# Hybrid attention and SSD layer: how the weights that combine three attention branches reach GpSimd

## The chip, the cores and the metric

The kernel runs on one core of a Trainium2 chip. The core has a matrix engine (PE, with its weight loads PEld), a vector engine (DVE), a scalar engine (ACT), GpSimd (POOL) and a sync engine (SP) that only issues DMAs; ACT and POOL can issue DMAs too, each in the order of its own queue. The metric is the device time of one execution in microseconds (us), the median of several runs.

## The reference, cut to what matters

One decoder layer, sequence 2048, width 1024, all in float32. A projection of the input gives queries, keys and values for 16 attention heads of size 64, two gates, and the inputs of a state-space mixer (SSD). Attention is computed three times, with dilations 1, 4 and 16, each over a window of 128 steps with a linear bias; each branch d gives an output o_d and a log-sum-exp l_d for every position and head. The three are combined:

```
o1, l1 = dilated_window_attention(q, k, v, slopes, DILATIONS[0])
o2, l2 = dilated_window_attention(q, k, v, slopes, DILATIONS[1])
o3, l3 = dilated_window_attention(q, k, v, slopes, DILATIONS[2])
wts = jax.nn.softmax(jnp.stack([l1, l2, l3], axis=0), axis=0)
y_att = wts[0] * o1 + wts[1] * o2 + wts[2] * o3
```

The result is gated and normalised, as is the SSD's; both are concatenated, multiplied by one output matrix, added to the input, and layer-normalised.

## The kernel before

**Stages.** First come the projections and the SSD (to 1168.5 us), which leave q, k, v, the gates and the SSD's output (d_us) in DRAM. Then the attention, 487.6 us, which the change is in, and the output projection, 383.9 us.

**Attention.** The loop runs over 8 pairs of heads (`pr`), and in each over 24 steps: three branches (`d` = 0, 1, 2), four quarters (`qd`), two halves. It is written as a pipeline by hand: iteration i issues `scores` of step i (matrix products into S, on DVE a fused bias, scale and row minimum, L945, and on ACT the exponential with its row sum, L951), `transposes` of step i-2 (PE to T, copied by DVE), and `values` of step i-3 (PE to N). After each second half, N is copied to `num`, the unnormalised output of the branch (L1016, L1019, L1022, all on ACT). Behind these stand, by the tables `STEPS` and `LOADS` and the conditions around them, jobs that are due at the step `at` = step i-3: loads for this pair and the next, and the combining of the pair before. The orders of PE, DVE, ACT and POOL are exactly those in which the program issues; only SP's queue is put in order by a planner.

**Statistics and weights.** Row minima and sums are gathered in a small tile. `statistics` transposes them and SP writes them to DRAM (d_st, L1038 to L1048), its last part at step (2,3,1). `gather` (L1050), a DMA on POOL's queue, reads them back as `cm`. In the next pair, at (0,2,1) and (0,3,0), `weights` makes the three softmax weights from cm: minimum, difference and exponential (part 0, L1057 to L1060), then products, sums, reciprocal (part 1, L1063 to L1067), all on DVE but the exponential. SP writes them to d_wd (L1068).

**Combining.** `combine(A, k)`, k from 0 to 5, works on tiles of 128 x 2048 elements, on POOL for pairs 0 to 6 and on DVE for the last. Steps 0, 1 and 3 broadcast the weights of a branch from d_wd to a tile `wb`, one row of 8 KB to 64 partitions, twice (L1081, on SP), and multiply `num` into it (L1083); steps 2 and 4 add (L1087); step 5 multiplies by the gate (L1098) and writes d_ua. Their places are in STEPS: 0 at (1,0,0), 1 at (1,1,0), 2 at (1,2,0), 3 at (1,3,0), 4 at (2,1,0), 5 at (2,2,0). Behind them POOL issues the next pair's loads: q, k (L862), v and vs (L878, L880). SP issues all six broadcasts as soon as d_wd has landed, since wb has three buffers. Then `permute` (L904, L908) copies the next pair's queries to the orders of branches 1 and 2, and the gather comes behind it in POOL's queue.

**Output projection.** 32 blocks, of the SSD's half (br = 1) and the attention's (br = 0), each multiplied with two halves of the output matrix: 64 products. Every block is first split in a high and a low part: `split` casts on ACT (L1141) and subtracts on DVE, for the very first block on POOL (L1143). `squares` makes its row sums for the norm (L1148, L1151). The first block's split is issued at (2,0,1) and (2,1,0) of the last pair. The weights of the last pair are made behind the attention (`weights(A, 0)`, `weights(A, 1)`), ahead of the loop over the products; the third block is split after product one, behind them in the order of ACT and DVE.

Of the kernel before, what the change touches and what calls it, by code (L numbers as in the profile page):

```python
# [9 lines left out]
F32 = mybir.dt.float32  # L10
# [6 lines left out]
S = 2048  # L17
# [11 lines left out]
def hybrid_layer(ctx, tc, xb, xc, w52, wv, wdt, convw, convb, dtb, alog, dskp, gcol, wout,  # L29
# [5 lines left out]
    def dap(t, off, ap):  # L35
        return bass.AP(tensor=t.tensor, offset=t.offset + off, ap=ap)
# [805 lines left out]
    with ExitStack() as c2:  # L842
# [137 lines left out]
        def values(A, d, qd, half, pts):  # L980

            pt, pc = pts
            if half == 0:
                if qd == 0:
                    A["num"].append(cm_.tile([128, NR, NJ], F32, name="num", bufs=6))
                A["N"] = [psN.tile([128, 512], F32, name=f"N{i}") for i in range(2)]
            num, v, vs = A["num"][d], A["v"][d], A["vs"].get(d)
            at = lambda bq: 4 * bq + qd if d == 1 else 4 * qd + bq
            out = lambda i, h, lo, hi: A["N"][i][64 * h:64 * h + 64, 128 * half + lo:128 * half + hi]

            def mm(o, l, r, start):
                nc.tensor.matmul(o, l, r, start=start, stop=True, skip_group_check=True)  # L992
            for i in range(2):
                m = at(2 * i + half)
                if first(d, qd, 2 * i + half):
                    for h in range(2):
                        mm(out(i, h, 0, 128), v[:, m, 64 * h:64 * h + 64], pt[:, h, i], half == 0)
                    continue
                for a in range(2):
                    for h in range(2):  # L1000
                        w = (v, vs)[a != i][:, m - (a == i == 0 or a != i), 64 * h:64 * h + 64]
                        mm(out(i, h, 64 * a, 64 * a + 64), w, pt[:, h, i, 64 * a:64 * a + 64], half == 0 and a == 0)
            for a in range(2):
                for i in range(2):
                    m, rows = at(2 * i + half), slice(64 * i, 64 * i + 64)
                    if first(d, qd, 2 * i + half):
                        continue
                    for h in range(2):
                        w = v[rows, m - i] if a == i else vs[rows, m - 2 * i]
                        mm(out(i, h, 64 * a, 64 * a + 64), w[:, 64 * h:64 * h + 64],  # L1010
                           pc[rows, h, 64 * a:64 * a + 64], False)
            if half == 1:
                for i in range(2):
                    nm = A["N"][i][:, 0:256]
                    if d == 0:
                        nc.scalar.copy(f2(num[:, 4 * qd + 2 * i:4 * qd + 2 * i + 2, :]), nm)  # L1016
                    elif d == 1:
                        o = num.rearrange("p (b s) (n a j) -> p n b a s j", b=4, a=2, j=16)[:, qd, 2 * i:2 * i + 2]
                        nc.scalar.copy(o, nm.rearrange("p (b a s j) -> p b a s j", b=2, a=2, s=4))  # L1019
                    else:  # L1020
                        j = 8 * (4 * qd + 2 * i)
                        nc.scalar.copy(num[:, :, j:j + 16].rearrange("p r (n j) -> p n r j", j=4),  # L1022
                                       nm.rearrange("p (n r j) -> p n r j", r=16, j=4))
# [28 lines left out]
        def weights(A, part):  # L1052

            m_, s_ = A["cm"][:, :, 0], A["cm"][:, :, 1]
            if part == 0:
                mm = A["mm"] = cm_.tile([128, 32], F32, name="mm")
                nc.vector.tensor_tensor(mm, m_[:, 0], m_[:, 1], op=OP.min)  # L1057
                nc.vector.tensor_tensor(mm, mm, m_[:, 2], op=OP.min)
                nc.vector.tensor_tensor(m_, mm[:, None, :].to_broadcast([128, 3, 32]), m_, op=OP.subtract)
                nc.scalar.activation(m_, m_, AF.Exp)  # L1060
                return
            mm = A["mm"]
            nc.vector.tensor_tensor(s_, s_, m_, op=OP.mult)  # L1063
            nc.vector.tensor_tensor(mm, s_[:, 0], s_[:, 1], op=OP.add)
            nc.vector.tensor_tensor(mm, mm, s_[:, 2], op=OP.add)
            nc.vector.reciprocal(mm, mm)
            nc.vector.tensor_tensor(m_, m_, mm[:, None, :].to_broadcast([128, 3, 32]), op=OP.mult)  # L1067
            nc.sync.dma_start(dap(d_wd[A["pr"]], 0, [[32, 128], [2 * S, 3], [1, 32]]), m_)  # L1068

        def combine(A, k):  # L1070

# [4 lines left out]
            pu = lambda a: a.rearrange("p (n r j) -> p r n j", r=NR, j=8)  # L1076
            if k in (0, 1, 3):
                d = k - k // 2
                wb = A["wb"] = cm_.tile([128, NR, NJ], F32, name="wb", bufs=3)
                for h in range(2):  # L1080
                    nc.sync.dma_start(f2(wb[64 * h:64 * h + 64]),  # L1081
                                      dap(d_wd[pr], (d * 2 + h) * S, [[0, 64], [1, S]]))
                eng.tensor_tensor(wb, A["num"][d], wb, op=OP.mult)  # L1083
                if k == 0:
                    A["acc"] = wb
            elif k < 5:
# [107 lines left out]
        def norm(n):  # L1194
# [10 lines left out]
            if n == 15:  # L1205
                for s in (slice(0, 512), slice(512, D)):
# [9 lines left out]

        O = {}
        pairs = {}
        STEPS = {(0, 0, 0): (None, "v", 0, 2), (0, 0, 1): (None, "vs", 0, 2), (1, 0, 0): (0, "q", 1),
                 (1, 1, 0): (1, "k", 1), (1, 2, 0): (2, "v", 1, 0), (1, 3, 0): (3, None, 0), (2, 0, 0): (None, "v", 1, 1),  # L1220
                 (2, 1, 0): (4, "vs", 1, 1), (2, 2, 0): (5, None, 0)}
        LOADS = {(0, 0, 0): ((8, None, "k_0"),), (1, 0, 1): ((9, None, "q_0"),), (1, 1, 0): ((10, None, "ex"),),
# [3 lines left out]
        todo = [(pr, d, qd, half) for pr in range(8) for d in range(3) for qd in range(4) for half in range(2)]  # L1226
        pts = {}
        TA = 2
# [1 line left out]
        with tc.manual_schedule(engines={E.PE, E.DVE, E.Activation, E.Pool}):  # L1230
            for i in range(len(todo) + TA + 1):
# [22 lines left out]
                if i > TA:  # L1254
# [5 lines left out]
                        statistics(pairs[pr], 1)  # L1260
                        gather(pairs[pr])
                    at = d, qd, half
                    if pr and at in ((0, 2, 1), (0, 3, 0)):
                        weights(pairs[pr - 1], qd - 2)
                    if at == (0, 0, 0) and pr < 7:
                        pairs[pr + 1] = load_pair(pr + 1)
                    if pr and at == (0, 3, 0):
# [42 lines left out]
            squares(0, 1)  # L1310
            split(1, 1)
            squares(1, 1)
            weights(A, 0)
            weights(A, 1)
            ops = [(n, 1) for n in range(4)] + [(n, 0) for n in range(4)]
            ops += [(n, br) for n in range(4, 16) for br in (1, 0)]
            items = [(4 * j + k, hf) for j in range(2) for k, hf in
# [5 lines left out]
            for i, (k, hf) in enumerate(items):  # L1323
# [19 lines left out]
                if i in splits:  # L1343
                    j = splits[i]
                    split(*ops[j])
                    squares(*ops[j])
                    for m in (j + 2,) if 4 < j < 30 else ():
                        fetch_raw(*ops[m])
                    if j >= 7 and j + 1 < 32 and ops[j + 1][1]:
                        residual(ops[j + 1][0])  # L1350
                        scaled(ops[j + 1][0])
# [97 lines left out]
```

## Time and profile before

| | us |
|---|---|
| median of 3 runs | 2043.36 (2038.81 to 2046.38) |
| profiled execution, its time | 2042.05 |
| its span, first to last instruction | 2040.3 |
| PE busy | 1961.6 (96%) |
| DVE busy | 1268.3 (62%) |
| ACT busy | 1125.5 (55%) |
| POOL busy | 1038.0 (51%) |
| mean granted clock | 0.986 |

A row of a group names the line, engine and operation, the tiles written and read, the shapes, the count, then busy time, mean duration in ns, and the idle time of the engine just before, with what ended it. A row of a timeline has start, duration, engine, line, operation, tiles, shape and count, and in brackets the idle time before it with its releaser. A row of the chain of waits has start, duration and what the time went to. "q" behind an engine's name is its queue.

### The profile page before, as it was taken

Reading aid. Unit: us, or ns where it says so; the run is one execution under the profiler, and the core shown is the slowest. Engines: PE = TensorE matmul, PEld = TensorE weight load, DVE = VectorE, ACT = ScalarE, POOL = GpSimd, SP = SyncE. Lnnn points to the kernel's source line nnn. Section 1 sums busy time; section 2 is a strip of 40 time slices with the busy share of each in tenths; the row PEclk is TensorE's granted clock in tenths of the full one; section 3 lists DMA queues with packets and bytes.
Section 4 is the critical chain, followed back from the end, with each engine's and each line's share of the span. In section 5 each row is a group of like instructions: output and inputs, shape, how many; then the busy total and the mean of one; then the engine's idle time right before and its main releaser. Section 6 shows DMA issues by size and latency. Waiting matters only on the chain.

```text
span 2040.3 us, 42723 instructions
## 1 busy us (share of the span) xinstructions
PE 1961.6 (96%) x16024; PEld 1598.5 (78%) x16024; DVE 1268.3 (62%) x3181; ACT 1125.5 (55%) x3067; POOL 1038.0 (51%) x881
## 2 busy tenths in 40 slices
PE   7999999999999999999999999999998889999998
PEld 6788888888888888988888766676666668888886
DVE  7455464677775666644454377887777756665553
ACT  4455443466565766456566488887878742222220
POOL 3466623666655667255655433668766662432222
PEclk8999999999999999999999999999999989999999
DMA  7478695466878777988888856777877799323220
GB/s 273 156 265 284 227 334 195 132 197 192 244 249 301 253 248 258 328 260 268 268 272 263 273 195 166 217 231 230 235 226 220 192 319 301 122 96 105 84 67 31
DMA packets 231150, 447.72 MB, mean 219 GB/s; under 512 B 40288, under 2 KB 112480, under 8 KB 219936
## 3 DMA queue, kind: packets, MB, share of 16 engines
q1 hardware_dynamic: 138928, 189.59, 29.5%
q0 software_dynamic: 43776, 160.49, 23.3%
q10 hardware_dynamic: 48240, 94.92, 15.1%
q8 instruction: 126, 2.06, 0.4%
q14 instruction: 80, 0.66, 0.1%
HBM read 301.91 MB, written 151.39 MB: 222 GB/s over the span
## 4 chain that ended last, share of the span: by engine, by line
PE 85%; DVE 5%; ACT 4%; DMA 3%; issue 2%; POOL 0%; SPq 0%; ACTq 0%; POOLq 0%; DVEq 0%
PE pp L251 13%; PE pp L255 13%; PE pp L253 13%; PE N L992 6%; PE S L939 5%; PE S L1175 4%; PE S L1177 4%; PE S L1176 4%; PE T L966 4%; PE pp L300 3%; ACT P L951 3%; PE ss L300 2%; PE T L1175 2%; PE T L1176 2%; PE T L1177 2%
## 5 line engine op out<-in xcount | busy, mean ns | idle before, releaser
L208 POOL TENSOR_TENSOR w<-wr,w 128x512 fp32r<-128x512 f32 x224 | 294.8, 1327 | 223.3 <-ACT w L207 195.1
L951 ACT ACTIVATE P<-P,st 128x192 f32<-128x192 f32 (+1 forms) x768 | 322.0, 421 | 71.7 <-DVE st L945 66.8
L243 ACT COPY ev<-pp 128x512 f32<-128x512 f32 x200 | 116.9, 587 | 318.1 <-PE pp L255 281.7
L945 DVE CUSTOM_DVE_ANT_0 P<-S,tb 128x192 f32<-128x192 f32 (+1 forms) x768 | 206.4, 324 | 101.6 <-PE S L939 72.6
L263 DVE TENSOR_TENSOR ev<-pp,ev 128x512 f32<-128x512 f32 x152 | 101.1, 686 | 147.9 <-PE pp L255 96.0
L1083 POOL TENSOR_TENSOR wb<-num,wb 128x2048 f32<-128x2048 f32 x21 | 95.5, 4549 | 114.7 <-DMA wb<-d_wd 65.5
L207 ACT CAST w<-wr 128x512 fp32r<-128x512 f32 x224 | 133.5, 619 | 22.0 <-issue 7.5
L951 ACT ACTIVATION_READ_ACCUMULATOR P<-P,st 128x1 f32 x768 | 144.3, 188 | 0.0
L992 PE MATMUL N<-PT,v 128*64 128x64 f32 (+1 forms) x1536 | 126.2, 261 | 11.8 <-ACT num L1016 8.5
L968 DVE COPY PT<-T 128x512 f32<-128x512 f32 x192 | 131.8, 686 | 4.4 <-PE T L966 4.4
L966 PE MATMUL T<-ident,P 128*128 128x128 f32 x768 | 128.4, 291 | 1.5 <-DVE st L945 1.2
L966 PEld LDWEIGHTS T<-ident,P 128*128 128x128 f32 x768 | 82.2, 143 | 49.2 <-issue 22.8
L939 PE MATMUL S<-k,ex 64*64 64x192 f32 (+1 forms) x2048 | 113.7, 333 | 5.8 <-issue 5.8
L202 DVE TENSOR_TENSOR wr<-wr 128x512 f32<-128x512 f32 x128 | 111.3, 870 | 11.3 <-DMA wr<-w 7.5
L992 PEld LDWEIGHTS N<-PT,v 128*64 128x64 f32 x1536 | 78.9, 138 | 49.5 <-issue 18.8
L454 DVE SCALAR_TENSOR_TENSOR ss<-U,cw,ss 128x512 f32<-128x512 f32 x144 | 106.0, 751 | 2.9 <-ACT ss L450 0.6
L1151 DVE TENSOR_REDUCE tb<-P 128x128 f32<-128x1024 f32 x30 | 60.2, 2005 | 45.4 <-ACT P L1148 23.0
L1213 POOL TENSOR_TENSOR k<-k,wb 128x1024 f32<-128x1024 f32 x8 | 25.8, 3225 | 122.5 <-DVE k L1212 122.5
L939 PEld LDWEIGHTS S<-k,ex 64*64 64x64 f32 x2048 | 69.2, 139 | 18.1 <-issue 11.8
L580 ACT ACTIVATE mt<-csb,cs 128x128 f32<-128x128 f32 x256 | 78.5, 393 | 0.9 <-PE ss L620 0.8
L589 DVE TENSOR_TENSOR mt<-mt,ss 128x1024 f32<-128x1024 f32 x32 | 39.0, 1219 | 54.6 <-ACT mt L585 54.3
L251 PE MATMUL pp<-TB11h,w 128*128 128x512 f32 x176 | 69.6, 395 | 0.0
(478 smaller groups left out, 6032.6 us busy)
## 6 DMA issues: line engine op xcount, KB each, us to landing
wr<-w ACTq DMA_DIRECT2D x164, 256.0 KB
d_wc<-w SPq DMA_DIRECT2D x48, 512.0 KB
w<-d_wc POOLq DMA_DIRECT2D x48, 512.0 KB, 6.2
wb<-d_wd SPq DMA_DIRECT2D x48, 512.0 KB
d_wo<-wot POOLq DMA_DIRECT2D x32, 512.0 KB, 4.3
csb<-d_cs ACTq DMA_DIRECT2D x32, 512.0 KB
v<-d_v POOLq DMA_DIRECT2D x16, 1024.0 KB, 6.8
vs<-d_v POOLq DMA_DIRECT2D x16, 960.0 KB, 8.6
```

The lines of the kernel that those rows point to most:

```text
L207: nc.scalar.copy(h, r)
L208: nc.gpsimd.tensor_tensor(l, r, h.bitcast(F32), op=OP.subtract)
L251: nc.tensor.matmul(ps, w[:, 0, k], th[:, k], start=start and k == 0, stop=False, skip_group_check=not start)
L253: nc.tensor.matmul(ps, w[:, 0, k], tl[:, k], start=False, stop=False, skip_group_check=not start)
L255: nc.tensor.matmul(ps, w[:, 1, k], th[:, k], start=False, stop=(k == 3), skip_group_check=not start)
L939: nc.tensor.matmul(o, A["q"][d][64 * h:64 * h + 64, blk, 64 * a:64 * a + 64], kv, start=True, stop=True)
L945: nc.vector.tensor_tensor_reduce(P[:, h, cs], sp[h][:, cs], t, -0.125, 3.0e38, OP.add, OP.min, accum_out=stat(A, 0, d, h, blk))
L951: nc.scalar.activation(p, p, AF.Exp, bias=stat(A, 0, d, h, blk), scale=-1.0, accum_out=stat(A, 1, d, h, blk))
L966: nc.tensor.transpose(tp[:, h, i], P[:, h, 256 * i:256 * i + 128], ident)
L968: nc.vector.tensor_copy(pt, tp)
L992: nc.tensor.matmul(o, l, r, start=start, stop=True, skip_group_check=True)
L1175: nc.tensor.matmul(ps, uh[:, e, :], wh, start=(e == 0), stop=False)
```

## The change

- The combining weights are made in three parts, at (0,2,1), (0,3,0) and (0,3,1). For pairs 0 to 6 the difference, the products, sums and the last multiplication run on POOL; the two minima and the reciprocal stay on DVE, the exponential on ACT.
- The broadcast is a function of its own. For pairs 0 to 6, the first is issued by SP right behind the weights, at (0,3,1). The multiplications of steps 0 and 1 are cut in two halves, and between the halves POOL issues the broadcast for the next multiplication. That of step 3 is whole.
- STEPS: the next pair's q, k and v come behind steps 1, 2 and 3 instead of 0, 1 and 2; steps 4 and 5 move to (2,0,0) and (2,0,1), ahead of v and vs, at (2,1,0) and (2,1,1). Two pairs of output weight loads move to (2,2,0) and (2,2,1).
- Of the two copies of N in branch 0, one goes to DVE.
- Behind the attention, the last pair's weights are made after product one and after the split of the third block, and ahead of its squares.

```diff
                     if d == 0:
-                        nc.scalar.copy(f2(num[:, 4 * qd + 2 * i:4 * qd + 2 * i + 2, :]), nm)
+                        copy = nc.vector.tensor_copy if i else nc.scalar.copy
+                        copy(f2(num[:, 4 * qd + 2 * i:4 * qd + 2 * i + 2, :]), nm)
...
+            eng = nc.vector if A["pr"] == 7 else nc.gpsimd
             if part == 0:
                 mm = A["mm"] = cm_.tile([128, 32], F32, name="mm")
                 nc.vector.tensor_tensor(mm, m_[:, 0], m_[:, 1], op=OP.min)
                 nc.vector.tensor_tensor(mm, mm, m_[:, 2], op=OP.min)
-                nc.vector.tensor_tensor(m_, mm[:, None, :].to_broadcast([128, 3, 32]), m_, op=OP.subtract)
+                eng.tensor_tensor(m_, mm[:, None, :].to_broadcast([128, 3, 32]), m_, op=OP.subtract)
+            mm = A["mm"]
+            if part == 1:
                 nc.scalar.activation(m_, m_, AF.Exp)
-                return
...
+                eng.tensor_tensor(s_, s_, m_, op=OP.mult)
+                eng.tensor_tensor(mm, s_[:, 0], s_[:, 1], op=OP.add)
+                eng.tensor_tensor(mm, mm, s_[:, 2], op=OP.add)
+            if part == 2:
+                nc.vector.reciprocal(mm, mm)
+                eng.tensor_tensor(m_, m_, mm[:, None, :].to_broadcast([128, 3, 32]), op=OP.mult)
+                nc.sync.dma_start(dap(d_wd[A["pr"]], 0, [[32, 128], [2 * S, 3], [1, 32]]), m_)
+
+        def broadcast(A, k):
+
+            d = k - k // 2
+            wb = A["w", k] = cm_.tile([128, NR, NJ], F32, name="wb", bufs=3)
+            for h in range(2):
+                (nc.sync if A["pr"] == 7 or k == 0 else nc.gpsimd).dma_start(
+                    f2(wb[64 * h:64 * h + 64]), dap(d_wd[A["pr"]], (d * 2 + h) * S, [[0, 64], [1, S]]))
...
             if k in (0, 1, 3):
                 d = k - k // 2
-                wb = A["wb"] = cm_.tile([128, NR, NJ], F32, name="wb", bufs=3)
-                for h in range(2):
-                    nc.sync.dma_start(f2(wb[64 * h:64 * h + 64]),
-                                      dap(d_wd[pr], (d * 2 + h) * S, [[0, 64], [1, S]]))
-                eng.tensor_tensor(wb, A["num"][d], wb, op=OP.mult)
+                if last:
+                    broadcast(A, k)
+                wb, num = A.pop(("w", k)), A["num"][d]
+                A["wb"] = wb
+                if last or k == 3:
+                    eng.tensor_tensor(wb, num, wb, op=OP.mult)
+                else:
+                    eng.tensor_tensor(wb[:, 0:8], num[:, 0:8], wb[:, 0:8], op=OP.mult)
+                    broadcast(A, 2 * k + 1)
+                    eng.tensor_tensor(wb[:, 8:16], num[:, 8:16], wb[:, 8:16], op=OP.mult)
...
-        STEPS = {(0, 0, 0): (None, "v", 0, 2), (0, 0, 1): (None, "vs", 0, 2), (1, 0, 0): (0, "q", 1),
-                 (1, 1, 0): (1, "k", 1), (1, 2, 0): (2, "v", 1, 0), (1, 3, 0): (3, None, 0), (2, 0, 0): (None, "v", 1, 1),
-                 (2, 1, 0): (4, "vs", 1, 1), (2, 2, 0): (5, None, 0)}
+        STEPS = {(0, 0, 0): (None, "v", 0, 2), (0, 0, 1): (None, "vs", 0, 2), (1, 0, 0): (0, None, 0),
+                 (1, 1, 0): (1, "q", 1), (1, 2, 0): (2, "k", 1), (1, 3, 0): (3, "v", 1, 0), (2, 0, 0): (4, None, 0),
+                 (2, 0, 1): (5, None, 0), (2, 1, 0): (None, "v", 1, 1), (2, 1, 1): (None, "vs", 1, 1)}
...
-                 (2, 0, 0): ((14, 0, "v"), (15, 0, "vs")), (2, 1, 0): ((12, 1, None), (13, 1, None)),
-                 (2, 1, 1): ((14, 1, None), (15, 1, None))}
+                 (2, 0, 0): ((14, 0, "v"), (15, 0, "vs")), (2, 2, 0): ((12, 1, None), (13, 1, None)),
+                 (2, 2, 1): ((14, 1, None), (15, 1, None))}
...
-                    if pr and at in ((0, 2, 1), (0, 3, 0)):
-                        weights(pairs[pr - 1], qd - 2)
+                    if pr and at in ((0, 2, 1), (0, 3, 0), (0, 3, 1)):
+                        weights(pairs[pr - 1], 2 * qd + half - 5)
+                    if pr and at == (0, 3, 1):
+                        broadcast(pairs[pr - 1], 0)
...
-            weights(A, 0)
-            weights(A, 1)
...
                     split(*ops[j])
+                    if i == 0:
+                        for n in range(3):
+                            weights(A, n)
                     squares(*ops[j])
```

More of the change, by code (lines that the diff above doesn't have):

```diff
@@ L1058, in weights @@
                 nc.vector.tensor_tensor(mm, mm, m_[:, 2], op=OP.min)
-                nc.vector.tensor_tensor(m_, mm[:, None, :].to_broadcast([128, 3, 32]), m_, op=OP.subtract)
+                eng.tensor_tensor(m_, mm[:, None, :].to_broadcast([128, 3, 32]), m_, op=OP.subtract)
+            mm = A["mm"]
+            if part == 1:
                 nc.scalar.activation(m_, m_, AF.Exp)
-                return
[L1062 to L1068, printed above, removed]
+                eng.tensor_tensor(s_, s_, m_, op=OP.mult)
[11 more added lines that the diff above has]
+                    f2(wb[64 * h:64 * h + 64]), dap(d_wd[A["pr"]], (d * 2 + h) * S, [[0, 64], [1, S]]))
         def combine(A, k):
```

## The prediction

> **What bounds the kernel now.** The run has three stages. I read first how the engines share them (busy time by stretches: total, then PE, PEld, DVE, ACT, POOL, each with its count of instructions, then granted clock, DMA share and GB/s): projections, the attention that the change is in, and the output projection.
>
> ```profile
> 1168.50:1656.10 487.60, 451.04 (x8224) 332.51 (x8223) 374.18 (x1898) 397.33 (x1761) 304.54 (x231) 0.97 0.76 223
> 1656.10:2040.00 383.90, 366.65 (x1608) 296.97 (x1601) 212.44 (x275) 93.90 (x132) 105.57 (x54) 0.98 0.39 124
> ```
>
> In the attention PE is busy for 451 of 488 us, so its bubbles look like the thing to win. The waits of PE in that stage:
>
> ```profile
> PE N L992 <- issue: 12.9, 6, 3.2
> PE N L992 <- ACT num L1016: 8.5, 7, 1.7
> PE S L939 <- issue: 5.8, 2, 3.2
> ```
>
> The "issue" rows (18.7 us) are stops in which PE waits for nothing that the profile shows; the other row is the weights' work, which delays a copy on ACT once a pair.
>
> But another engine runs nearly as long a loop. The timeline of GpSimd (POOL) over one pair's combining, with the idle time before a row and its releaser in brackets:
>
> ```profile
> 1500.24 4.51 POOL L1083 TENSOR_TENSOR wb<-num,wb 128x2048 f32<-128x2048 f32 x1 [15.38 <-DMA wb<-d_wd]
> 1504.69 0.60 POOL L862 DMA_DIRECT2D q<-d_q  x1
> 1506.00 4.53 POOL L1083 TENSOR_TENSOR wb<-num,wb 128x2048 f32<-128x2048 f32 x1 [0.71 <-DMA wb<-d_wd]
> ...
> 1529.71 4.55 POOL L1098 TENSOR_TENSOR wb<-wb 128x2048 f32<-128x2048 f32 x1
> 1534.21 2.79 POOL L904 COPY ex<-q 128x256 f32<-128x256 f32 x8
> 1536.96 2.28 POOL L908 COPY ex<-q 128x512 f32<-128x512 f32 x4
> 1542.68 0.87 POOL L1050 DMA_DIRECT2D cm<-d_st  x1 [3.44 <-DVE st L945]
> ```
>
> From 1500.24 to 1539.24 POOL hardly stops: six combining operations of 4.5 us, loads that it issues, two permutes. Only then can it issue the gather of the statistics (cm, L1050), since its queue runs in order. And the gather closes a loop:
>
> ```profile
> 1542.68 3.19 DMA cm<-d_st
> 1603.73 4.56 DMA cm<-d_st
> 1549.37 0.38 SPq L1068 DMA_DIRECT2D d_wd<-cm  x1
> 1553.44 3.68 SPq L1081 DMA_DIRECT2D wb<-d_wd  x6
> ```
>
> The first two rows, two pairs' gathers, are from the chain of waits, the others from the DMA issues of SP. The gather lands, the weights are made and written (1549.37), read back broadcast (1553.44), and the next pair's combining starts. One turn of POOL's own loop, from gather to gather, is 1603.73 - 1542.68 = 61.05 us; at the end of the turn before, 3.44 were left over, waiting for the statistics. Over the stage the slack is this row's:
>
> ```profile
> L1050 POOL DMA_DIRECT2D cm<-d_st x7 | 6.1, 865 | 34.4 <-DMA d_st<-sT 16.8 <-DVE st L945 15.5 <-DVE PT L968 2.1
> ```
>
> The 16.8 us are the first pair's, with no combining before it. The other six turns have 15.5 + 2.1 = 17.6 us, 2.9 us each. **So POOL's loop stands 2.9 us a pair behind the path that sets the end.** Whatever adds more than that to POOL's queue lengthens every pair, since VectorE (DVE), which holds the weights in its own order, stops at cm and with it the whole pipeline.
>
> **The change part by part.** *Broadcasts on POOL's queue.* The second and third broadcast (two issues each) go from SP to POOL. An issue costs POOL 0.6 us by the L862 row (8 KB a partition, as here): 4 x 0.6 = 2.4 us a pair, on the loop.
>
> *The wait that they make.* The second broadcast is issued in the middle of the first multiplication, so its transfer is covered by the issues (1.2 us) and the second half (4.51 / 2 = 2.3 us), 3.5 us in all; then the next multiplication needs it. How long does it take? No broadcast was issued on POOL before, so it is bounded:
>
> ```profile
> 1613.49 3.67 SPq L1081 DMA_DIRECT2D wb<-d_wd  x6
> ...
> 1621.08 4.55 POOL L1083 TENSOR_TENSOR wb<-num,wb 128x2048 f32<-128x2048 f32 x1 [15.92 <-DMA wb<-d_wd]
> DMA to landing us min/median/max: 6.5/8.5/12.8
> ```
>
> The same megabyte issued by SP, first in its queue, let POOL start 1621.08 - 1613.49 = 7.6 us after the issue. A megabyte issued on POOL (q and k, the last row, all issues of L862) took 6.5 at least, 8.5 in the median. I take 7.6, the same transfer: a wait of 7.6 - 3.5 = 4.1 us; ends 3.0 and 5.0, and 9.3 by the slowest. In place of it goes the wait of 0.71 that stands before the second multiplication now: -0.7. The third broadcast is issued one multiplication, one add and q's and k's issues ahead (1.2 + 2.3 + 0.6 + 4.6 + 0.6 = 9.3 us): hidden; at 12.8 it would cost 3.5.
>
> *Halves.* Four half operations in place of two whole ones. Nearest rows:
>
> ```profile
> L208 POOL TENSOR_TENSOR w<-wr,w 128x512 fp32r<-128x512 f32 x224 | 294.8, 1327 | 223.3 <-ACT w L207 195.1
> L1083 POOL TENSOR_TENSOR wb<-num,wb 128x2048 f32<-128x2048 f32 x21 | 95.5, 4549 | 114.7 <-DMA wb<-d_wd 65.5
> L1213 POOL TENSOR_TENSOR k<-k,wb 128x1024 f32<-128x1024 f32 x8 | 25.8, 3225 | 122.5 <-DVE k L1212 122.5
> ```
>
> A half is 2.27 by its own row, 2.65 as two of the first row, 3.2 by the last. I take its own, with 0.05 for a second start: +0.2 a pair (ends +1.5 and +3.8).
>
> *Weights on POOL, spread over three steps.* The five small operations fall where POOL idles (the 15.4 us before L1083), so they don't lengthen its queue; what counts is that d_wd is written one step later, about 1.9 us (half of the 3.8 us that two steps of the first dilation take below). In pairs 2 to 6 that is covered: d_wd to the first broadcast took 1553.44 - 1549.37 = 4.1 us there, against 1613.49 - 1611.80 = 1.7 in the last pair, whose v and vs loads come later; so up to 2.4 us of it is queueing behind those loads that the later write skips. If the cover is gone it costs 1.9 a turn. In the last pair it counts.
>
> *Copies of the first dilation shared with DVE.* Two steps of it, and a copy of that size on DVE:
>
> ```profile
> 1240.90:1244.70 3.80, 3.72 (x62) 2.55 (x60) 3.12 (x19) 3.77 (x19) 0.76 (x1) 1.00 0.87 265
> L977 DVE COPY PC<-T 128x256 f32<-128x256 f32 x98 | 40.7, 416 | 1.7 <-PE T L974 1.5
> ```
>
> ACT is full (3.77 of 3.80), PE nearly (3.72), DVE has 0.68 free for a 0.4 us copy. So PE takes over the bound after 0.1 us; four such stretches a pair, 0.4 us. It counts for the first pair alone; later it only makes DVE reach cm sooner.
>
> *Keys, queries, values later; combining steps 4 and 5 sooner.* The order on POOL is the same work: q and k each behind one more multiplication or add, v and vs behind step 5 instead of between. k's issue comes some 20 us into a chain of 45, early enough for the next pair. No term of its own. The six broadcasts no longer fill the queues at one stroke, which could end the "issue" stops; but time that PE gains there it spends waiting for cm, which POOL's loop sets.
>
> *Sum of a turn:* 2.4 + 4.1 - 0.7 + 0.2 = 6.0 us. Six turns: 36.0, less the slack 17.6, less 0.4: the last pair's gather comes **18.0 us later**, at 1621.7 instead of 1603.73.
>
> *The last pair.* The split of the first output block leaves its low part to POOL (L1143). It stood ahead of steps 4 and 5; these now come before it.
>
> ```profile
> 1647.49 2.37 POOL L1143 TENSOR_TENSOR num<-ex,num 128x1024 fp32r<-128x1024 f32 x1 [0.73 <-ACT num L1141]
> 1649.83 4.54 POOL L1087 TENSOR_TENSOR wb<-wb 128x2048 f32<-128x2048 f32 x1
> ...
> 1657.21 4.65 POOL L1098 TENSOR_TENSOR wb<-wb 128x2048 f32<-128x2048 f32 x1
> 1662.15 1.23 POOL L1099 DMA_DIRECT2D d_ua<-wb  x1 [0.30 <-POOL wb L1098]
> ```
>
> From the first multiplication to the end of that split it was 1649.86 - 1621.08 = 28.8 us. Added: 4.5 + 4.7 + 1.5 for steps 4, 5 and the write, 2.4 for issues, 0.2 for halves, 1.1 of wait (the v, vs and weight issues there cover more of the 7.6), less the 0.7 before it: 42.5. The first multiplication came 1621.08 - 1603.73 = 17.35 after the gather, now 1.9 later: 1621.7 + 19.25 + 42.5 = 1683.5. The first output product needs it:
>
> ```profile
> 1656.16 0.48 PE L1175 MATMUL S<-k,num 128*128 128x512 f32 x1
> 1661.98 0.48 PE L1175 MATMUL S<-k,num 128*128 128x512 f32 x1
> 1676.41 0.79 PE L1175 MATMUL S<-k,ex 128*128 128x512 f32 x1 [7.91 <-ACT ex L1141]
> 1684.47 0.47 PE L1175 MATMUL S<-k,num 128*128 128x512 f32 x1
> ```
>
> These rows start products one, two, three and four. The sooner split of block three removes the 7.91 us ahead of the third. But product one, from its third matrix multiplication on 5.3 us, now ends at 1683.5 + 5.3 + 2.2 (after an idle stretch a product takes 8.06 us, the third row to the fourth, instead of 5.82) = 1691.0, the next two at 5.8 each: the fourth starts at 1702.6, 18.1 us later than now. The last pair's weights stand in DVE's order behind product one's root and move with it, so that gain is spent here too. The profiled execution took 2042.05 us (span 2040.3): 2042.05 + 18.1 = 2060.2, **2060 us**; it lies 1.3 us under the runs' median of 2043.36.
>
> The Trainium skill (DMA: Bandwidth & Descriptors, section Anatomy of one DMA — SWDGE (gpsimd) path) gives a load from GpSimd's queue 2.0 us plus its bytes over 436 GB/s, 4.4 us for a megabyte by estimate. By that, the wait would be 0.6 + 4.4 - 3.5 = 1.5 us, the turn 3.4, the six turns 20.4 - 18.0 = 2.4 more, and the run about 2044. The rows above, 6.5 at least and 7.6 for this very broadcast, speak against it.
>
> **The rivals.** *Dearer issues and halves:* landing 8.5, halves 2.65 each: 2.4 + 5.0 - 0.7 + 1.5 = 8.2 a turn, 49.2 - 18.0 = 31.2 later: 2073. For it: q's loads shared the queues too. Against: with one broadcast at a time less is in flight.
>
> *Level, by a cheaper start:* the cover of the later d_wd works as a gain. One broadcast alone ahead of the multiplication and d_wd written after the v loads save the 2.4 us of queueing, and the landing is the fastest, 6.5: 2.4 + 3.0 - 0.7 + 0.2 - 2.4 = 2.5 a turn, 15.0 - 18.0 = -3.0; the split on POOL then ends at 1662.5, the fourth product starts at 1681.6: 2039. Against: in five turns the v loads, not d_wd, set when the first broadcast goes.
>
> *Faster, the other side:* the second broadcast lands within the 3.5 us that cover it (it decides from there), and the 2.4 are saved: 2.4 - 0.7 + 0.2 - 2.4 = -0.5 a turn. With the "issue" stops gone PE no longer sets the loop either, and the slack of 18.0 is gained with 3.0 for the turns: gather at 1582.7, POOL's split at 1644.5, the fourth product at 1663.6, 20.9 sooner: 2021. For it: the stops come while broadcasts fill the queues. Against: 6.5 us is the least that any such load took.
>
> **How the numbers follow.** A measurement of this kernel tells 0.5%, about 10 us, from no change: faster is under 2033, slower over 2053.6. Forecast 0.50, of which 0.08 ends within 0.5% (a wait of 3.0 takes 6.6 off); dearer 0.16; level 0.21; faster 0.13. Slower: 0.42 + 0.16 = 0.58; same 0.08 + 0.21 = 0.29; faster 0.13. The forecast's own range is 2052 (wait 3.0) to 2073; the range down to 2038 takes in the level case, and up to 2085 the slow ends (halves 3.2, landing 8.5: 10.5 a turn, 45 later, nearly).
>
> **What would show it.** In the profile after: half multiplications of 2.3 us; POOL idle some 4 us ahead of the second multiplication, released by the broadcast; the gather's idle of 3 us gone; DVE idle several us ahead of L1057 in each pair, on cm; gathers 64 us apart; L1143 on POOL near 1683 and PE waiting there. Wrong it would be if the gather still waits for the statistics, or if the second multiplication follows at once.

## The result and the profile after

The changed kernel takes **2116.06 us** (median of 4 runs, 2112.79 to 2118.72), the kernel before 2041.91 in runs beside it (4 runs, 2038.81 to 2046.38): ratio 1.0354, 95% interval 1.0329 to 1.0379. The forecast was 2060, 18 us more than before; it is 74 us more. The sign was right and the size four times too small.

The stages first (busy time by stretches: total, then PE, PEld, DVE, ACT, POOL, granted clock, DMA share, GB/s), after:

```profile
1168.50:1721.50 553.00, 456.30 (x8078) 336.13 (x8079) 372.65 (x1881) 388.12 (x1718) 320.10 (x299) 0.91 0.63 189
1721.50:2116.90 395.40, 374.17 (x1747) 302.71 (x1747) 214.74 (x289) 99.38 (x146) 119.70 (x63) 0.98 0.41 131
```

and the kernel before, cut at the same points of its work (the last scores of the last pair):

```profile
1168.50:1649.10 480.60, 444.25 (x8079) 326.97 (x8078) 370.00 (x1884) 394.23 (x1750) 297.54 (x227) 0.97 0.75 220
1649.10:2040.30 391.20, 373.45 (x1751) 302.51 (x1747) 216.62 (x289) 97.00 (x145) 112.57 (x58) 0.98 0.40 129
```

The attention is 72.4 us longer, the output projection 4.2. So the loss is in the six turns from gather to gather. One of them on POOL's timeline, after (start, duration, in brackets the idle time before):

```profile
1312.53 0.86 POOL L1051 DMA_DIRECT2D cm<-d_st  x1 [7.63 <-DMA tb<-tabs]
...
1331.02 2.37 POOL L1097 TENSOR_TENSOR wb<-num,wb 128x1024 f32<-128x1024 f32 x1 [11.06 <-DMA wb<-d_wd]
1333.33 1.14 POOL L1078 DMA_DIRECT2D wb<-d_wd  x2
1334.48 2.40 POOL L1099 TENSOR_TENSOR wb<-num,wb 128x1024 f32<-128x1024 f32 x1
1341.19 2.37 POOL L1097 TENSOR_TENSOR wb<-num,wb 128x1024 f32<-128x1024 f32 x1 [4.31 <-DMA wb<-d_wd]
...
1352.07 0.58 POOL L862 DMA_DIRECT2D k<-d_k  x1
...
1364.39 4.56 POOL L1114 TENSOR_TENSOR wb<-wb 128x2048 f32<-128x2048 f32 x1
1368.90 1.20 POOL L880 DMA_DIRECT2D v<-d_v  x1
1370.10 1.23 POOL L880 DMA_DIRECT2D vs<-d_v  x1
1371.31 2.79 POOL L904 COPY ex<-q 128x256 f32<-128x256 f32 x8
1374.05 2.27 POOL L908 COPY ex<-q 128x512 f32<-128x512 f32 x4
1383.97 0.86 POOL L1051 DMA_DIRECT2D cm<-d_st  x1 [7.65 <-DMA tb<-tabs]
```

From gather to first multiplication 18.5 us, from there to the end of the second permute 45.3, then 7.65 of idle: 71.4. The wait before the second multiplication is there (4.31), the halves take 2.37 and 2.40. What the forecast didn't have is the last row: POOL has done its queue and the gather waits *longer* than before, not less. In the groups by line:

```profile
L1051 POOL DMA_DIRECT2D cm<-d_st x7 | 6.0, 858 | 65.8 <-DMA d_st<-sT 34.3 <-DMA tb<-tabs 31.5
L939 PE MATMUL S<-k,q 64*64 64x128 f32 x1024 | 45.6, 296 | 45.0 <-DMA k<-d_k 43.7 <-DVE ev L263 1.4
```

the second of them before:

```profile
L939 PE MATMUL S<-k,q 64*64 64x128 f32 x1024 | 41.7, 278 | 1.4 <-DVE ev L263 1.4
```

and among PE's waits after (total, times, longest):

```profile
PE S L939 <- DMA k<-d_k: 43.7, 6, 7.9
PE N L992 <- DVE PT L968: 27.3, 5, 6.0
PE T L966 <- ACT sT L1036: 11.7, 1, 11.7
PE S L1193 <- POOL num L1159: 11.3, 1, 11.3
```

The gather's idle is 65.8 us, against 34.4 before. (The releaser is inferred; the table load tb shares SP's queue with d_st. In the packet records, d_st's last packet ends 1.5 us before the gather of the timeline above.) And PE, whose scores with q lost 1.4 us in all before and none of it to keys, now waits 43.7 us for them, at the start of each pair from the third on. The third row is a single stop, in the fourth turn, where SP issued the first part of the statistics (1512.59) right behind d_ua (1512.14).

I use one table for all runs. Its first three columns are parts of a turn, each a mean of six turns, worked out from POOL's timeline as just done: gather to first multiplication, from there to the end of the second permute (POOL's chain), idle before the next gather. The fourth is their sum, the fifth the median time beside the kernel before (2041.91, 2040.73, 2041.15 and 2040.26 in the four comparisons).

| run | to first mult. | chain | idle | turn | time, us | ratio (95%) |
|---|---|---|---|---|---|---|
| before | 19.0 | 38.9 | 2.9 | 60.9 | 2041 | |
| after | 19.5 | 45.3 | 8.2 | 73.0 | 2116.06 | 1.0354 (1.0329 to 1.0379) |
| steps_back | 18.8 | 45.3 | 2.4 | 66.6 | 2081.36 | 1.0198 (1.0163 to 1.0232) |
| steps_only | 18.7 | 39.4 | 8.1 | 66.3 | 2074.58 | 1.0167 (1.0145 to 1.0189) |
| qk_back | 18.8 | 45.2 | 6.6 | 70.6 | 2105.91 | 1.0324 (1.0305 to 1.0343) |
| qk_dua | 20.7 | 47.7 | 0.0 | 68.3 | 2095.20 | 1.0274 (1.0252 to 1.0296) |
| sb_sp | 19.6 | 39.2 | 3.2 | 61.9 | 2050.12 | 1.0044 (1.0027 to 1.0060) |
| sb_defer | 19.0 | 45.2 | 0.0 | 64.2 | 2069.72 | 1.0139 (1.0119 to 1.0160) |
| so_defer | 20.4 | 39.4 | 3.7 | 63.5 | 2059.52 | 1.0087 (1.0072 to 1.0102) |
| swap_only | 18.7 | 39.2 | 8.2 | 66.1 | 2073.31 | 1.0158 (1.0143 to 1.0173) |
| bf_defer | 20.9 | 39.1 | 0.9 | 60.8 | 2040.89 | 1.0009 (0.9998 to 1.0021) |
| sb_act | 23.2 | 38.7 | 0.0 | 61.9 | 2053.24 | 1.0072 (1.0059 to 1.0085) |

After against before, unrounded: chain +6.3, idle +5.2, the rest +0.5: 12.1 a turn, six turns 72.5.

### The profile page after: what moved, and what is told of

Same layout as the page of the kernel before. It is cut to its first block, busy times and chain, and to the rows that moved or that the text cites. A ratio compares the mean times of both kernels' runs of the same rounds, so it can differ in the third digit from the quotient of the medians.

```text
span 2116.9 us, 42763 instructions
## 1 busy us (share of the span) xinstructions
PE 1973.8 (93%) x16024; PEld 1607.2 (76%) x16024; DVE 1269.2 (60%) x3178; ACT 1124.0 (53%) x3037; POOL 1067.5 (50%) x958
## 4 chain that ended last, share of the span: by engine, by line
PE 69%; DMA 14%; DVE 6%; POOL 5%; ACT 3%; issue 3%; SPq 1%; ACTq 0%; POOLq 0%; DVEq 0%
PE pp L251 13%; PE pp L255 12%; PE pp L253 12%; DMA wb<-d_wd 6%; PE S L1191 3%; PE pp L300 3%; PE S L1193 3%; PE S L1192 3%; DMA d_st<-sT 2%; DMA k<-d_k 2%; PE ss L300 2%; PE N L992 2%; PE S L939 2%; PE T L1191 2%; PE T L1193 2%
## 5 line engine op out<-in xcount | busy, mean ns | idle before, releaser
L992 PE MATMUL N<-PT,v 128*64 128x64 f32 (+1 forms) x1536 | 130.1, 268 | 34.6 <-DVE PT L968 27.3
L992 PEld LDWEIGHTS N<-PT,v 128*64 128x64 f32 x1536 | 83.4, 143 | 71.6 <-DVE PT L968 28.5
L939 PE MATMUL S<-k,ex 64*64 64x192 f32 (+1 forms) x2048 | 113.8, 334 | 1.3 <-issue 1.3
L939 PE MATMUL S<-k,q 64*64 64x128 f32 x1024 | 45.6, 296 | 45.0 <-DMA k<-d_k 43.7
L1097 POOL TENSOR_TENSOR wb<-num,wb 128x1024 f32<-128x1024 f32 x14 | 33.2, 2370 | 101.1 <-DMA wb<-d_wd 101.1
L939 PEld LDWEIGHTS S<-k,ex 64*64 64x64 f32 x2048 | 68.7, 139 | 15.6 <-issue 8.0
L939 PEld LDWEIGHTS S<-k,q 64*64 64x64 f32 x1024 | 30.0, 142 | 54.3 <-issue 42.2
```

What stands on the lines that cost most here:

```text
L939: nc.tensor.matmul(o, A["q"][d][64 * h:64 * h + 64, blk, 64 * a:64 * a + 64], kv, start=True, stop=True)
```

## The experiments

**Which half of the change?** *steps_back* is the change with the old STEPS and LOADS; *steps_only* is the kernel before with the new ones.

The diff is steps_back's against the change; steps_only's against the kernel before is the same with the signs exchanged (LOADS as in the change's diff).

```diff
-        STEPS = {(0, 0, 0): (None, "v", 0, 2), (0, 0, 1): (None, "vs", 0, 2), (1, 0, 0): (0, None, 0),
-                 (1, 1, 0): (1, "q", 1), (1, 2, 0): (2, "k", 1), (1, 3, 0): (3, "v", 1, 0), (2, 0, 0): (4, None, 0),
-                 (2, 0, 1): (5, None, 0), (2, 1, 0): (None, "v", 1, 1), (2, 1, 1): (None, "vs", 1, 1)}
+        STEPS = {(0, 0, 0): (None, "v", 0, 2), (0, 0, 1): (None, "vs", 0, 2), (1, 0, 0): (0, "q", 1),
+                 (1, 1, 0): (1, "k", 1), (1, 2, 0): (2, "v", 1, 0), (1, 3, 0): (3, None, 0), (2, 0, 0): (None, "v", 1, 1),
+                 (2, 1, 0): (4, "vs", 1, 1), (2, 2, 0): (5, None, 0)}
```

> The changed kernel with the old tables STEPS and LOADS: keys, queries, values and combining steps 4 and 5 stand where they were; single broadcasts, halves, weights on GpSimd, the copy on DVE and the sooner split stay. Theory 1 (the forecast's own term: the wait for the second broadcast and the issues lengthen GpSimd's queue by 6.0 us a pair, of which 2.9 were slack): gathers 63 to 65 us apart, 2050 to 2060 us. Theory 2 (moving keys and steps is the whole loss): the same spacing as before, 61 us, 2035 to 2043. Theory 3 (the loss is in the broadcasts on GpSimd's queue whatever the order): over 2090.

> The kernel before with the new tables alone; all broadcasts by SP at one stroke, whole multiplications, weights on DVE. Theory A (k's late load is the loss): k's issue comes some 15 us after the first multiplication instead of 10, and lands still in time, so gathers stay 61 to 62 us apart: 2040 to 2055. Theory B (d_ua, v and vs now fall together with the statistics' round trip through DRAM and delay the gather): gathers 64 to 68 us apart, 2060 to 2085.

Both halves cost nearly the same: +40.6 (2081.36) and +33.9 (2074.58) against 2040.73, together 74.5, the whole loss. In the table they are the two parts: steps_back has the long chain and the old idle time, steps_only the old chain and the long idle time. Neither takes from the other. For steps_only that is theory B. For steps_back it is none of the three: its time lies between the ranges of theories 1 and 3, and its turn, 66.6 us, over the 63 to 65 expected.

**Is it the keys, or the write in front?** *qk_back* is the change with q and k issued behind combining steps 0 and 1 again; *qk_dua* adds to it that d_ua of every pair is issued on POOL's queue. The first diff is qk_back's, against the change, the second what qk_dua adds.

```diff
-        STEPS = {(0, 0, 0): (None, "v", 0, 2), (0, 0, 1): (None, "vs", 0, 2), (1, 0, 0): (0, None, 0),
-                 (1, 1, 0): (1, "q", 1), (1, 2, 0): (2, "k", 1), (1, 3, 0): (3, "v", 1, 0), (2, 0, 0): (4, None, 0),
+        STEPS = {(0, 0, 0): (None, "v", 0, 2), (0, 0, 1): (None, "vs", 0, 2), (1, 0, 0): (0, "q", 1),
+                 (1, 1, 0): (1, "k", 1), (1, 2, 0): (2, None, 0), (1, 3, 0): (3, "v", 1, 0), (2, 0, 0): (4, None, 0),
```

```diff
-                (nc.gpsimd if pr == 6 else nc.sync).dma_start(dap(d_ua, pr * 128, [[7 * 128, 128], [128 * 7 * 128, 16], [1, 128]]),
+                nc.gpsimd.dma_start(dap(d_ua, pr * 128, [[7 * 128, 128], [128 * 7 * 128, 16], [1, 128]]),
```

> The changed kernel with the next pair's q and k issued behind steps 0 and 1 as before; everything else as changed. Theory A (PE waits 8 us for k at each pair's start, and that wait is in the loop): gathers fall from 71.5 to about 64 us apart, 2065 to 2075. Theory B (the statistics stand behind d_ua in SP's queue, which leaves when step 5 ends, and behind d_ua, v and vs in the DMA engines): PE no longer waits for k but waits as much for cm; gathers 70 to 72 apart, 2100 to 2116.

> As qk_back, and d_ua is written from GpSimd's queue for every pair, so that nothing of step 5 stands ahead of the statistics in SP's queue. Theory A: no difference to qk_back but 1.2 us of issue a pair. Theory B, queue order: the statistics leave when they are ready, gathers 64 to 66 apart, 2065 to 2075. Theory B, DMA engines: they leave sooner but land behind d_ua, v and vs as late as in qk_back.

The keys are worth 10 us: PE's wait for them falls to 11.9 us in all, but 54.8 us (27.3 in the change) are then spent on DVE, which waits 58.1 us for cm (30.1 in the change). Most of PE's wait for keys was spare time that the late gather gave it. With d_ua off SP's queue the gather never waits (0.0), worth another 11, though the write costs elsewhere: POOL's chain is 47.7 (its issue there takes 1.2 us, and POOL stands 0.75 ahead of it), and the way to the first multiplication 20.7 instead of 18.8. So neither theory's range holds: queue order, which foretold 64 to 66 us a turn and 2065 to 2075, is right about the gather and wrong about the time.

**The wait for the second broadcast, and the slack.** *sb_sp* is steps_back with all three broadcasts issued by SP behind the weights, as before (halves, weights on POOL, shared copies and sooner split stay). *sb_defer* is steps_back with d_ua of the six pairs whose write SP issues (0 to 5) issued by ACT at (0,2,0) of the pair that follows its combining. Both diffs are against steps_back.

```diff
-                        broadcast(pairs[pr - 1], 0)
+                        for k in (0, 1, 3):
+                            broadcast(pairs[pr - 1], k)
...
-                    broadcast(A, 2 * k + 1)
...
-                (nc.sync if A["pr"] == 7 or k == 0 else nc.gpsimd).dma_start(
+                nc.sync.dma_start(
```

```diff
-                (nc.gpsimd if pr == 6 else nc.sync).dma_start(dap(d_ua, pr * 128, [[7 * 128, 128], [128 * 7 * 128, 16], [1, 128]]),
-                                  u.rearrange("p (n t) -> p n t", t=128))
+                A["u"] = u
+                if pr == 6:
+                    write(A, nc.gpsimd)
+
+        def write(A, queue):
+
+            queue.dma_start(dap(d_ua, A["pr"] * 128, [[7 * 128, 128], [128 * 7 * 128, 16], [1, 128]]),
+                            A["u"].rearrange("p (n t) -> p n t", t=128))
...
+                    if pr > 1 and at == (0, 2, 0):
+                        write(pairs[pr - 2], nc.scalar)
```

> The change with the old order of combining steps and loads (as in the run steps_back), and with all three broadcasts issued by SP right behind the weights, as before; the halves, the weights on POOL, the shared copies and the sooner split stay. If the wait for the second broadcast and POOL's four issues carry that run's +40 us, POOL's chain from the first multiplication to the last permute falls from 45.0 to about 39.5 us, gathers stand 61 to 62 us apart and the run takes 2035 to 2050 us. If the weights written a step later, or the halves, carry it, the chain still falls but gathers stay 64 us or more apart and the run stays over 2065 us.

> The change with the old order of combining steps and loads (as steps_back), and the write of the combined output (d_ua) of pairs 1 to 5 taken out of SP's queue: it is issued by ACT in the next pair's third step, long after POOL has finished it, so that the statistics' writes never stand behind it. If the lost slack is SP's queue (d_st behind d_ua behind POOL's last combining step), the gather's idle of 1.6 to 3.2 us before it falls to zero, gathers stand 63 to 64 us apart instead of 66 and the run takes 2065 to 2071 us. If the statistics are late by themselves, since PE and DVE were stopped by the late weights, the gather goes on waiting 2 us or more and the run stays at 2078 to 2085 us.

sb_sp: 2050.12, so POOL's issues and the wait for the broadcast are 31 of the 40 us. What is left, 9 us, holds the halves, the weights' new place, the shared copies and the sooner split together (the chain is 0.2 longer than before, the turn 1.0). Of these only the split was tried alone: 3 us of loss (tail_only, below). sb_defer: 2069.72, 12 us less than steps_back, with POOL never idle at the gather:

```profile
L1051 POOL DMA_DIRECT2D cm<-d_st x7 | 6.1, 865 | 16.8 <-DMA d_st<-sT 16.8
```

(The 16.8 is the first pair's.) Its turn of 64.2 us is the one that the prediction forecast, 61.05 + 6.0 - 2.9 = 64.15. So the forecast's turn exists, but only where d_ua doesn't stand ahead of the statistics. The time of sb_defer is still 29 us over the kernel before, not 18: in the profiled execution the last gather comes 22.6 us later than before (1626.30), and the part behind it is 8.1 longer, for which the forecast had 0.1. In steps_back d_ua does stand ahead of them; the timeline there, all engines, at the end of a turn:

```profile
1360.67 0.26 ACT L1036 COPY sT<-T 64x128 f32<-64x128 f32 x1
1367.58 0.36 SPq L1115 DMA_DIRECT2D d_ua<-wb  x1
1368.04 4.91 SPq L1045 DMA_DIRECT2D d_st<-sT  x4
1370.21 2.27 POOL L908 COPY ex<-q 128x512 f32<-128x512 f32 x4
...
1374.89 0.87 POOL L1051 DMA_DIRECT2D cm<-d_st  x1 [2.42 <-DMA tb<-tabs]
```

The statistics are ready at 1360.93, but SP, whose queue is served in order, issues them only at 1368.04, behind d_ua, which waits for POOL's last combining step. In all six turns of steps_back they stand ready for 7.1 to 8.2 us; before, they were issued within 0.03 us. When POOL's chain grows, the statistics grow late with it, and POOL's own permutes (5 us) are too short to cover their way.

**Which move of the new order?** *swap_only* is the kernel before with steps 4 and 5 ahead of the second dilation's v and vs; nothing else is moved but the two later output weight loads. *so_defer* is steps_only with d_ua on ACT, by sb_defer's diff. Swap_only's diff against the kernel before (LOADS as in the change's diff):

```diff
-                 (1, 1, 0): (1, "k", 1), (1, 2, 0): (2, "v", 1, 0), (1, 3, 0): (3, None, 0), (2, 0, 0): (None, "v", 1, 1),
-                 (2, 1, 0): (4, "vs", 1, 1), (2, 2, 0): (5, None, 0)}
+                 (1, 1, 0): (1, "k", 1), (1, 2, 0): (2, "v", 1, 0), (1, 3, 0): (3, None, 0), (2, 0, 0): (4, None, 0),
+                 (2, 0, 1): (5, None, 0), (2, 1, 0): (None, "v", 1, 1), (2, 1, 1): (None, "vs", 1, 1)}
```

> The kernel before with one move alone: combining steps 4 and 5 ahead of the second dilation's loads v and vs, as in the change; the next keys, queries and first values stay at their old places. If d_ua, v and vs together on the statistics' round trip carry the +34 us of steps_only, this run has most of it: gather idle 6 us or more, 2062 to 2078 us. If the later keys, queries and values carry it, it stays at 2038 to 2050 us.

> The kernel before with only the new order of combining steps and loads (as steps_only), and d_ua issued by ACT in the next pair's third step. If d_ua, ahead of the statistics in SP's queue and in the DMA engines, is what makes the gather late there, its idle of 8 us falls to 3 to 5 us (v and vs are still in the engines), gathers stand 62 to 63 us apart instead of 66 and the run takes 2050 to 2062 us. If the two loads v and vs alone carry the delay, the gather still waits 7 us or more and the run stays over 2068 us.

swap_only has 32 of the 34 us; the later keys, queries and first values add next to nothing to the kernel before (in the change, with its longer chain, keys and queries are 10). The end of a turn in swap_only, all engines:

```profile
1356.62 1.20 POOL L880 DMA_DIRECT2D v<-d_v  x1
1356.71 0.36 SPq L1099 DMA_DIRECT2D d_ua<-wb  x1
1357.18 3.12 SPq L870 DMA_DIRECT2D tb<-tabs  x1
1357.82 1.21 POOL L880 DMA_DIRECT2D vs<-d_v  x1
1358.84 0.26 ACT L1035 COPY sT<-T 64x128 f32<-64x128 f32 x1
...
1360.39 3.24 SPq L1044 DMA_DIRECT2D d_st<-sT  x4
1361.77 2.28 POOL L908 COPY ex<-q 128x512 f32<-128x512 f32 x4
...
1372.31 0.86 POOL L1050 DMA_DIRECT2D cm<-d_st  x1 [8.26 <-DMA tb<-tabs]
```

and the same place before:

```profile
1351.50 0.37 SPq L1099 DMA_DIRECT2D d_ua<-wb  x1
1353.14 0.26 ACT L1035 COPY sT<-T 64x128 f32<-64x128 f32 x1
1353.42 3.15 SPq L1044 DMA_DIRECT2D d_st<-sT  x4
1354.15 2.27 POOL L908 COPY ex<-q 128x512 f32<-128x512 f32 x4
1358.56 0.87 POOL L1050 DMA_DIRECT2D cm<-d_st  x1 [2.14 <-DVE PT L968]
```

Before, the way from the statistics on ACT (done 1353.40) to the gather takes 5.2 us (5.2 to 7.9 in the six turns); v and vs have been issued long ahead, the later one at 1345.67. In swap_only some three megabytes, v, vs and d_ua, start within 1.2 us, just ahead of it, and the way takes 1372.31 - 1359.10 = 13.2 (12.2 to 13.7). The trace's packet records show where: d_st is 1024 packets of 32 bytes, issued from 1360.39 on, and the first of them moves at 1368.22. Until 1363 it is d_ua's 512-byte packets that move, ahead of them in the same queue, and then v's and those of the table tb, which SP issued between d_ua and d_st. From d_st's first issue to its last packet, swap_only takes 10.1 to 11.6 us in the six turns, the kernel before 4.0 to 6.2.

Taking d_ua out of SP's queue (so_defer; the table, too, is then not between) gives back 15 of the 34 us; the idle falls from 8.1 to 3.7, not to zero, and d_st takes 4.2 to 9.9 us. In the longest of these turns the first small packet moves at once (1354.49), but the last ends at 1363.58, while v and vs move. Behind the gather a part is lost again: 20.4 us to the first multiplication instead of 18.7, with d_ua now moving there. How the 18 us that so_defer still loses divide between v and vs ahead of the gather and d_ua behind it was not tried apart.

**A version that beats both?** Four runs. *bf_defer* is the kernel before with d_ua on ACT, as in sb_defer but at (0,1,0). *tail_only* is the kernel before with the sooner split of the third block alone. *bf_mix* has both and the shared copies. *sb_act* is steps_back with d_ua on ACT at (0,1,1), and the second and third broadcast issued by ACT. The first diff is tail_only's, the second what sb_act has beside d_ua.

```diff
-            weights(A, 0)
-            weights(A, 1)
...
                     split(*ops[j])
+                    if i == 0:
+                        weights(A, 0)
+                        weights(A, 1)
```

```diff
-                (nc.sync if A["pr"] == 7 or k == 0 else nc.gpsimd).dma_start(
+                (nc.sync if A["pr"] == 7 or k == 0 else nc.scalar).dma_start(
...
-                    broadcast(A, 2 * k + 1)
...
+                    if pr and at in ((1, 0, 1), (1, 1, 1)):
+                        broadcast(pairs[pr - 1], 2 * qd + 1)
```

> The kernel before with one edit: the combined output's write (d_ua) of pairs 1 to 5 leaves SP's queue and is issued by ACT in the next pair's second step (0.45 us of ACT each). If d_ua ahead of the statistics' writes holds the gather back in the kernel before too, its idle of 2.1 to 3.4 us falls under 1.5 us, gathers stand 59 to 60 us apart instead of 61 and the run takes 2028 to 2036 us. If the gather there waits for the statistics themselves (PE and DVE set the turn), idle and spacing stay and the run takes 2038 to 2044 us.

> The kernel before with the sooner split of the third output block alone: the last pair's weights stand behind that split instead of ahead of it. If nothing takes the 7.9 us stop ahead of the third product back, the run is 5 to 8 us faster: 2033 to 2036 us. If the weights that are now later take it back (first multiplication of the last pair later, products that need them later), the stop moves and the run stays at 2038 to 2044 us.

> The kernel before with d_ua issued by ACT (as bf_defer), the sooner split (as tail_only) and the first dilation's copies shared between ACT and DVE. If the first two gains stand and add, 2020 to 2031 us; if one of them is nothing, 2030 to 2037 us; if the copies on DVE make its column of work the bound, 2040 us or more.

> The change with the old order of combining steps and loads, the second and third broadcast issued by ACT in the second dilation's second and fourth step (so each goes singly, lands before POOL needs it and costs POOL no issue), and d_ua issued by ACT. If POOL's issues, the wait and SP's queue were the whole harm, POOL's chain is 39 to 40 us, the gather hardly waits, the stops of PE that the profile names issue are shorter than 6 us in all, gathers stand 59 to 61 us apart and the run takes 2020 to 2036 us. If ACT, full in the first dilation, pays for the issues, PE waits for ACT's P or num and the run takes 2045 us or more.

None does. bf_defer is level (1.0009, 0.9998 to 1.0021), though its gather hardly waits: idle 0.9 a turn instead of 2.9, as expected if d_ua held it; the 2028 to 2036 us expected with it don't come. In the DMA issues (count, size, median us from issue to landing) stands why, before and in bf_defer:

```profile
cm<-d_st POOLq DMA_DIRECT2D x7, 96.0 KB, 2.9
cm<-d_st POOLq DMA_DIRECT2D x7, 96.0 KB, 5.6
```

The gather lands 5.6 us after its issue instead of 2.9, since d_ua now moves beside it (in the first turn, which has no d_ua, it takes 2.7). Two microseconds won ahead of the gather are lost behind it. tail_only is slower by 0.2% (1.0023, 1.0012 to 1.0034): the 7.9 us stop is gone, and two of its PE waits are new or grown:

```profile
PE S L1177 <- DVE num L1143: 4.6, 2, 4.1
PE N L1183 <- DVE tb L1151: 3.4, 1, 3.4
```

bf_mix, at 1.0028 (1.0014 to 1.0043), shows no gain of the shared copies either. sb_act has the short chain and no idle, but 23.2 us from gather to first multiplication, 4.2 more than before, and ends at 2053.24, far from the 2020 to 2036 expected. Its trace sorts the six turns: in four, ACT's first broadcast is issued between SP's two, and from SP's first to the first multiplication it takes 12.0 to 13.1 us; in two it is issued behind both, and it takes 7.4 and 7.8 (18.8 and 19.5 from the gather). d_ua doesn't sort them: it is issued 3 to 5 us ahead of the gather in two of the long turns and in both short ones. No run changed that order alone.

## Why the prediction was wrong, point by point

- **Terms of the chain: right.** Issues: 1.14 and 1.09 us for two each, 2.2 for the 2.4 forecast. Wait: 4.31 in the timeline above, 4.1 forecast. The Trainium skill (DMA: Bandwidth & Descriptors, section Anatomy of one DMA — SWDGE (gpsimd) path) would have given 1.5; the measurement decides for the row of the kernel's own broadcast. Halves: 2.37 and 2.40 for 2.27 and some. Sum: +6.3 a turn for 6.0. Weights a step later: 18.8 us from gather to multiplication in steps_back for 19.0, covered as said.
- **"Six turns: 36.0, less the slack 17.6": wrong, first failed step.** I read the idle time ahead of the gather as slack that a longer POOL queue could eat. It is slack only if what the gather waits for stays where it is. But that write stood behind d_ua in SP's queue, and d_ua waits for POOL's last combining step: what was waited for moves with the waiter. The rows were there (d_ua at L1099, right behind L1098; the gather, which reads d_st). In steps_back the idle stays at 2.4 and the time goes up by 40.6, near the 36 without the subtraction; sb_defer, with d_ua out of that queue, gains 12 of it back.
- **"No term of its own" for steps 4 and 5 sooner, v and vs later: wrong, second failed step, 34 us.** I counted POOL's issues, found the same number of them, and didn't ask where the three megabytes travel at that time. v and vs went from some 13 and 8 us ahead of the statistics' writes to just before them, and the statistics' small writes, in the loop of every turn, wait for them. swap_only shows it alone: +32.
- **"k's issue … early enough for the next pair": wrong in result, small in effect.** k went 21 us into the chain, as forecast, and PE waited 43.7 us for it in all; the way back in qk_back is worth 10.
- **The last pair: right in mechanism, of little weight.** PE waits for POOL's split (L1159) 11.3 us and the 7.9 us stop is gone; the stage behind the attention is 4.2 us longer. The forecast let the part behind the last gather grow by 0.1 us; it grew by 4.3 after, and by 8.1 in sb_defer. That the sooner split gains nothing, tail_only confirms.
- **The "issue" stops** did go, as allowed for: 18.7 us in two rows before, 2.7 in the same two after. The time was spent at cm, as forecast, and at k, which was not.
- **The rivals** all shared the subtraction of the slack; so none came near. The "dearer" one reached 2073 by dearer terms, which the runs don't show. Missing was the case in which the gather's data grow late with POOL.

## What to carry to other kernels

Before idle time is subtracted as slack, follow what the waiting instruction waits for back through its queue: if anything ahead of it there waits for the engine that gets slower, the slack can move away with it. A moved load costs more than its issue: look which small transfer on the loop is issued in the microseconds after it, and count the bytes that it will share the DMA engines with. Two changes that are each off the path by the same margin can both be on it, and then their costs add.

## What the runs showed of the hardware

- **Small packets beside large ones.** From the first to the last, d_st's 1024 packets of 32 bytes take 1.4 to 2.2 us in the six turns before (the shortest is the one shown, 1356.03 to 1357.45), and 2.1 to 9.1 us in so_defer, where v and vs are in flight from another queue (the longest is the one shown, 1354.49 to 1363.58). The Trainium skill (DMA: Bandwidth & Descriptors, section Queues, rings and completion order) says that each DMA engine takes turns between the queues, a packet at a time. That longest turn agrees: the small writes start 0.8 us after their issue, ahead of v's first packet, and then advance among the large ones. Four of the six don't: there the first small packet moves 3.6 to 3.9 us after its issue, with no other data in its own queue and v's moving in the other. In swap_only, with d_ua and the table ahead in their own queue, they wait 7.8 us for their first turn.
- **"issue" stops of PE and broadcasts that overlap.** In the rows PE N L992 and S L939 <- issue they sum to 18.7 us before and to 24.5 in sb_sp, where SP issues six broadcasts at one stroke, and to 22.8 in sb_act, where ACT issues the last four within 6.3 us of SP's two. Where POOL issues them 10 us apart they are 2.7 (after) and 5.6 us, the two rows of sb_defer:

```profile
PE N L992 <- issue: 3.5, 5, 1.0
PE S L939 <- issue: 2.1, 2, 1.4
```

  More waiting elsewhere doesn't remove them: steps_only, whose PE waits 26.1 us for DVE in the row N L992 <- DVE PT, has 18.8. That the overlap causes them is the reading these runs fit; no run tested it alone.
- **The granted clock was lower where PE waited more, and once without that.** From 1168.5 to 1640 us it was 0.97 before and in sb_sp, 0.96 in sb_defer, 0.95 in swap_only, 0.93 in qk_back and 0.92 after. Over the whole attention the same 8078 or so matrix multiplications took 456.3 us after and 444.3 before, some 3% more; that this lengthened the turns was not shown. Against it stands tail_only, whose profiled execution has 0.92 in that stretch too, with PE busy for 441.2 of the 471.5 us (435.1 before): it took 2049.35 us, among its runs of 2039.50 to 2051.76. Over the whole run it has 0.934, the others of tail_only 0.98 to 0.99.
